# Gathers of tokens that fill all 128 partitions, in a transformer layer with a sorted mixture of experts

## The chip, the cores and the metric

The kernel runs on one core of one Trainium2 chip. The metric is device time in microseconds, from the start of the program to its end; the time before is the median of three runs. One further execution was taken by the hardware profiler, and all rows below come from it.

## The reference

Two transformer blocks follow each other on 512 tokens of 1024 features, all in float32. The first has an attention part (two kinds of heads) and a mixture of 32 experts; the second has another two kinds of attention. The part that matters here is the mixture:

```python
logits = (hf @ router_w + router_b)
top_val, top_idx = lax.top_k(logits, TOP_K)            # 4 of 32 experts for each token
gate = jax.nn.softmax(top_val, axis=-1)
...
u = hf[toks] @ w1[e] + b1[e]                           # 1024 -> 2048, for the tokens of expert e
g_, lin = u[:, :D_FF], u[:, D_FF:]
g_ = jnp.minimum(g_, SWIGLU_LIMIT)
lin = jnp.clip(lin, -SWIGLU_LIMIT, SWIGLU_LIMIT)
y = ((lin + 1.0) * g_ * jax.nn.sigmoid(SWIGLU_ALPHA * g_)) @ w2[e] + b2[e]   # 1024 -> 1024
return y * wts[:, None]
...
out = jax.ops.segment_sum(y.reshape(R, D), row_tok, num_segments=T)
```

For each expert its tokens are gathered, sent through two matrices, and added back into the rows that they came from.

## The kernel before

The first half of the program computes the attention of the first block, the router and, in `middle`, the lists of tokens of each expert. `h2d` is a table in DRAM with the normalised tokens (512 rows of 1024 numbers, 4 KB each), `accd` the one into which results are added.

**Experts.** Experts 0 and 1 come first; the other 30 are sorted by how many tokens they have, and the sorted order is dealt out so that small and large experts alternate (`KIND`, line 39): 15 small ones with up to 64 tokens ("S"), and 17 large ones ("L"). `SLOTS` (line 45) is the number of rows that an expert's tiles have: 64 for a small expert, 128 for the first two and the four largest of the others, 96 for the remaining 11 large ones. Tokens that do not fit go to `overflow`, a loop at the end that runs for no expert here.

**The stream of weights.** Every expert has 8 MB of first and 4 MB of second weights, loaded in pieces of 1024 KB by the SP queue (`Stream.pump`, line 135) into free blocks of SBUF. A load is issued as soon as a block is free, in the order in which the weights are used, so the queue runs ahead of the matmuls. Each piece for a large expert is split into two parts (a cast on ACT, line 167, and a subtraction on DVE, line 168) and used by three matmuls per tile (`mm3`, lines 257 to 259). A small expert's weights are used as they land, in full float32 matmuls that work on two halves of the output side by side (`pair`, line 1592).

**One expert.** The loop at line 1742 takes them in order. In the turn of expert e the kernel multiplies with the first weights of e (`up`), then with the second weights of e-1 (`down`). Between the pieces of `up` a hook runs: at the second piece the activations of e-1 are transposed (`turn_a`), at the fifth the gathered tokens of e+1 are transposed into the layout of the matmuls (`turn_x`), and right behind that the gather of expert e+2 is issued on GpSimd's queue (`gather`, line 1600) into the same tile `xg`. So a gather has about one expert's time until it is needed. At the end of `down` GpSimd issues a scatter that adds the result's rows to `accd` (line 1734 for large experts, whole rows; line 1705 for small ones, two halves of a row on 128 partitions).

**The gather before.** It reads whole rows of 4 KB, as many as the expert has slots, into as many partitions:

```python
ix = self.ig[0:n, c:c + 1] if large(e) else self.igs[0:n, c - NL:c - NL + 1]
nc.gpsimd.indirect_dma_start(out=xg[0:n, :], out_offset=None, in_=self.h2d[0:T, :], ...)
```

For a small expert `turn_x` then transposes eight pieces of 64 rows (line 1625) into one bank, which ACT copies to `small_x` with the eight pieces in order; `up` reads piece k at column 64 k. `igs`, the list of rows for small experts, is made once in `sorted_tables` (line 1495).

Of the kernel before, what the change touches and what calls it, by code (L numbers as in the profile page):

```python
# [14 lines left out]
OP = mybir.AluOpType  # L15
# [4 lines left out]
P = 128  # L20
T = 512
NT = 4
D = 1024
KD = 8
# [13 lines left out]
NL = E - 2 - NSMALL  # L38
# [6 lines left out]
SLOTS = [64 if KIND[_p] == "S" else P if _p < 2 or COL[_p] < NWIDE else 96 for _p in range(E)]  # L45
# [142 lines left out]
class Build:  # L188
# [1278 lines left out]
    def sorted_tables(self, pp):  # L1467

        nc = self.nc
        mm = nc.tensor.matmul  # L1470
        ns = E - 2
        y = pp.tile([P, D], F32, name="y", bufs=1)
        tu = self.sb_.cols(T, 2 * P)
        ones = self.halves[0:32, 0:1]

        def turned():
            nc.tensor.transpose(y[0:96, 0:P], self.tt, self.ident)
            nc.vector.tensor_copy(tu[0:96, 0:P], y[0:96, 0:P])
            nc.vector.tensor_copy(tu[0:96, P:].rearrange("p (h s) -> p h s", h=2),
                                  y[0:96, None, 0:64].to_broadcast([96, 2, 64]))  # L1480

        def by_rank():
            mm(y[:, 512:608], lhsT=tu[0:96, 0:P], rhs=self.bd[0:96, :], start=True, stop=True)
            mm(y[:, 608:704], lhsT=tu[0:96, P:], rhs=self.bd[0:96, :], start=True, stop=True)
            mm(y[0:1, 704:736], lhsT=self.pidf[0:32, :], rhs=self.bd[0:32, 0:E], start=True, stop=True)
            mm(y[0:1, 736:768], lhsT=ones, rhs=self.g[0:32, :], start=True, stop=True)
            nc.vector.tensor_copy(self.ids, y[0:1, 704:736])

        def lists():
            t, t2 = [y[:, a:a + 96].rearrange("p (c e) -> p c e", c=3) for a in (512, 608)]  # L1490
            f = self.sb_.cols(6 * T // 4 + 2 * E, NSMALL)

            nc.vector.tensor_scalar(f, t2[:, 1, NL:ns], -1.0, 1.0, op0=OP.mult, op1=OP.add)
            nc.vector.tensor_scalar(f, f, self.far2, self.half, op0=OP.mult, op1=OP.add)
            nc.vector.tensor_copy(self.igs, t2[:, 0, NL:ns])
            nc.vector.scalar_tensor_tensor(self.iscs, t2[:, 0, NL:ns], 2.0, f, op0=OP.mult, op1=OP.add)
            nc.vector.tensor_copy(self.gates, t2[:, 2, NL:ns])
            self.slots(t[:, 0, :NL], t[:, 1, :NL], t[:, 2, :NL], self.sb_.cols(6 * T // 4 + 3 * E, NL), self.ig[:, :NL],
                       self.isc[:, :NL], self.gate[:, :NL])

        def slots():
            r, a, b = [self.sb_[0:1, 6 * T // 4 + o:6 * T // 4 + o + E] for o in (0, E, 2 * E)]
            nc.vector.tensor_copy(r, y[0:1, 736:768])
            nc.vector.tensor_scalar(a, r, float(NL), -32.0, op0=OP.is_ge, op1=OP.mult)
            nc.vector.tensor_scalar(b, r, float(NWIDE), -32.0, op0=OP.is_ge, op1=OP.mult)
            nc.vector.tensor_tensor(out=a, in0=a, in1=b, op=OP.add)
            nc.vector.tensor_scalar(r, r, float(ns), 64.0, op0=OP.is_ge, op1=OP.mult)
            nc.vector.tensor_tensor(out=a, in0=a, in1=r, op=OP.add)
            nc.vector.tensor_scalar(a, a, 128.0, None, op0=OP.add)
            nc.vector.tensor_copy(self.cap, a)  # L1510
            nc.vector.tensor_tensor(out=a, in0=self.cntf[0:1, :], in1=a, op=OP.subtract)
            nc.vector.tensor_scalar(a, a, 0.0, None, op0=OP.max)
            nc.vector.tensor_copy(self.over, a)
            nc.vector.tensor_reduce(out=self.top, in_=a, axis=AX.X, op=OP.max)
        return [turned, by_rank, lists, slots]
# [30 lines left out]
    def experts(self):  # L1546
        nc, I, st, ar = self.nc, self.I, self.st, self.ar
        mm = nc.tensor.matmul
        with ExitStack() as cx:
# [18 lines left out]
            g_, l_ = [w[1].cols(q * D, D) for q in range(2)]  # L1568
            bb = self.bb
            sels = [bb.cols(FF + D // 2 + q * P, P) for q in range(3)]  # L1570
            accs = self.accd[:, :].rearrange("t (h n) -> (t h) n", h=2)

            def large(e):
                return KIND[e] == "L"
# [13 lines left out]
            def pair(out, lhsT, rhs, last):  # L1588

                for h in range(2):  # L1590
                    o = slice(64 * h, 64 * h + 64)
                    mm(out[o, :], lhsT=lhsT, rhs=rhs[:, h * 512:(h + 1) * 512], start=False, stop=last,  # L1592
                       tile_position=(0, 64 * h), skip_group_check=True)
            u_ = {}

            def gather(e):
                c = COL[e]
                n = SLOTS[e]
                ix = self.ig[0:n, c:c + 1] if large(e) else self.igs[0:n, c - NL:c - NL + 1]
                nc.gpsimd.indirect_dma_start(out=xg[0:n, :], out_offset=None, in_=self.h2d[0:T, :],  # L1600
                                             in_offset=bass.IndirectOffsetOnAxis(ap=ix, axis=0))

            def halves(e, at, H, L):
# [9 lines left out]
            a8 = s_.rearrange("p (j m o) -> p j o m", j=4, o=2)  # L1613
            a4 = s_[:, 0:T].rearrange("p (j m o) -> p j o m", j=2, o=2)

            def turn_x(e):
                def at(j):
                    return xg[:, j * P:(j + 1) * P]

                if large(e):  # L1620
                    halves(e, at, xH[e], xL[e])
                else:
                    p = pp.tile([P, D], F32, name="tr", bufs=1)
                    for j in range(KD):
                        nc.tensor.transpose(p[:, j * 64:j * 64 + 64], at(j)[0:64, :], self.ident[0:64, 0:64])
                    nc.scalar.copy(small_x, p[:, 0:T])
                self.select(sels[e % 3], e)

# [10 lines left out]
            def up(e, hook):  # L1639
                u = u_[e] = pp.tile([P, 2 * FF], F32, name="u", bufs=1)  # L1640
                m = SLOTS[e]
                if not large(e):
                    for b in range(2):
                        bias2(u[:, b * 512:(b + 1) * 512], e, b * 512)
                    for k, n in enumerate(self.e_w1[e]):
                        st.at = n
                        v = st.view(n)
                        for b in range(2):
                            pair(u[:, b * 512:(b + 1) * 512], small_x[:, k * 64:k * 64 + 64],
                                 v[:, 0, b * D:(b + 1) * D], k == KD - 1)  # L1650
                        st.free(n)
                        st.ahead(st.split_to)
                        hook(k)
                    return
                for c in range(4):
                    bias(u[0:m, c * 512:(c + 1) * 512], e, c % 2, (c // 2) * 512)
                for k in range(KD):
                    for h, p in enumerate(self.e_w1[e][k]):
                        st.at = st.pieces[p][0]
                        st.ahead(p)  # L1660
                        H, L = st.take(p)
                        for q in range(2):
                            c = 2 * h + q
                            s = slice(q * 512, (q + 1) * 512)
                            self.mm3(u[0:m, c * 512:(c + 1) * 512], xH[e][:, k, 0:m], xL[e][:, k, 0:m], H[:, 0, s],
                                     L[:, 0, s], False, k == KD - 1)
                        st.done(p)
                    hook(k)
# [14 lines left out]
            def down(e):  # L1683
# [4 lines left out]
                if not large(e):  # L1688
                    y = y[:, 0:T]
                    bias2(y, e, FF)  # L1690
                    for k in range(KD):
                        n = self.e_w2[e][k // 2]
                        st.at = n
                        o = (k % 4) * P + (k // 4) * 64
                        pair(y, small_a[:, o:o + 64], st.view(n)[:, k % 2, :], k == KD - 1)
                        if k % 2:
                            st.free(n)
                            st.ahead(st.split_to)
                        self.step()
                        if e == E - 2 and k == KD // 2:  # L1700
                            turn_a(E - 1)
                    ys = l_[:, 0:T]
                    c -= NL
                    nc.vector.scalar_tensor_tensor(ys, y, self.gates[:, c:c + 1], g2s, op0=OP.mult, op1=OP.mult)
                    nc.gpsimd.indirect_dma_start(
                        out=accs, out_offset=bass.IndirectOffsetOnAxis(ap=self.iscs[:, c:c + 1], axis=0), in_=ys,
                        in_offset=None, compute_op=OP.add)
                    return
# [720 lines left out]
```

## Time and profile before

| | us |
|---|---|
| median of three runs | 1778.27 |
| lowest and highest run | 1773.07, 1780.42 |
| the profiled execution | 1769.57 |
| its span in the trace | 1767.8 |
| TensorE (PE) busy in it | 1655.4 (94%) |
| DVE busy | 1101.6 (62%) |
| ACT busy | 847.1 (48%) |
| GpSimd (POOL) busy | 382.8 (22%) |

A busy TensorE is not one at its peak, since its matmuls are pipelined and overlap in the records. The profile's slices show in which part of the program each engine and the transfers are busy, its windows the same for any stretch, with the rate at which all transfers together moved bytes (GB/s) and the mean share in which the 16 DMA engines were busy; that share counts each packet's time and can read a little above 1 where packets overlap. The experts take the stretch from about 410 to 1475 us of the span.

### The profile page before, as it was taken

How to read it: one execution, taken by the hardware profiler on the slowest of the kernel's cores; microseconds unless marked ns; L12 is line 12 of the kernel's file. 1: busy time of each engine (PE TensorE's matmuls, PEld its weight loads, DVE VectorE, ACT ScalarE, POOL GpSimd, SP SyncE). 2: the span in 40 equal slices, each digit the busy share in tenths (PEclk: the TensorE clock that was granted, in tenths of full speed). 3: DMA queues.
4: the chain of work that ended last, by engine and by line, in shares of the span. 5: the costliest groups of instructions: out<-in, count | busy, mean ns of one | idle time of the engine just before them, and what ended most of it. 6: DMA issues, size and time to landing. Idle time of an engine off the chain costs nothing. (4 is left out here: it accounts for less than half of the span.)

```text
span 1767.8 us, 22276 instructions
## 1 busy us (share of the span) xinstructions
PE 1655.4 (94%) x8017; PEld 1066.5 (60%) x8018; DVE 1101.6 (62%) x1741; ACT 847.1 (48%) x1321; POOL 382.8 (22%) x259
## 2 busy tenths in 40 slices
PE   6999998897999999999999999999999989999998
PEld 4677755576775565464455464455455456778887
DVE  2567668669776475475485475476476486476653
ACT  4356568425554254254254255245245253477571
POOL 3013234222011121330321231231231130210120
PEclk9999999999999999999999999999999999999999
DMA  9802045457799999999999999999999996100301
GB/s 363 310 35 72 1 151 187 167 220 276 282 392 410 398 413 412 391 405 412 394 411 411 394 409 411 391 410 413 390 410 412 394 369 245 44 28 24 119 1 48
DMA packets 99656, 505.11 MB, mean 286 GB/s; under 512 B 10962, under 2 KB 20258, under 8 KB 48338
## 3 DMA queue, kind: packets, MB, share of 16 engines
q1 hardware_dynamic: 89972, 477.94, 67.3%
q0 software_dynamic: 8944, 24.63, 5.5%
q8 instruction: 65, 1.06, 0.2%
q10 hardware_dynamic: 624, 1.06, 0.2%
q14 instruction: 51, 0.42, 0.1%
HBM read 485.75 MB, written 17.84 MB: 285 GB/s over the span
## 5 line engine op out<-in xcount | busy, mean ns | idle before, releaser
L168 DVE TENSOR_TENSOR b<-b,b 128x1024 fp32r<-128x1024 f32 (+1 forms) x474 | 557.3, 1221 | 281.1 <-ACT b L167 280.4
L167 ACT CAST b<-b 128x1024 fp32r<-128x1024 f32 (+1 forms) x476 | 472.2, 1044 | 219.4 <-DMA b<-in_exp_w 175.9
L1734 POOL DMA_INDIRECT accd<-b,isc x16 | 162.1, 10130 | 440.7 <-DVE b L1729 440.7
L257 PE MATMUL z<-b,b 128*128 128x512 f32 (+1 forms) x544 | 224.9, 413 | 2.9 <-ACT b L167 2.1
L257 PE MATMUL u<-b,b 128*96 128x512 f32 (+1 forms) x560 | 224.5, 401 | 0.0
L259 PE MATMUL u<-b,b 128*96 128x512 f32 (+1 forms) x560 | 220.0, 393 | 0.0
L258 PE MATMUL u<-b,b 128*96 128x512 f32 (+1 forms) x560 | 219.8, 392 | 0.0
L1592 PE MATMUL u<-b,b 128*64 128x512 f32 x960 | 216.5, 597 | 0.8 <-DMA b<-in_exp_w 0.8
L258 PE MATMUL z<-b,b 128*128 128x512 f32 (+1 forms) x544 | 210.7, 387 | 1.5 <-DVE b L168 1.5
L259 PE MATMUL z<-b,b 128*128 128x512 f32 (+1 forms) x544 | 210.4, 387 | 0.0
L1592 PEld LDWEIGHTS u<-b,b 128*64 128x64 f32 x960 | 64.5, 136 | 122.1 <-issue 112.3
L257 PE MATMUL y<-b,b 128*96 128x512 f32 (+1 forms) x256 | 109.7, 428 | 23.6 <-ACT b L167 23.4
L258 PE MATMUL y<-b,b 128*96 128x512 f32 (+1 forms) x256 | 110.8, 433 | 20.2 <-DVE b L168 19.1
L257 PEld LDWEIGHTS z<-b,b 128*128 128x128 f32 x544 | 103.0, 189 | 33.5 <-issue 13.4
L257 PEld LDWEIGHTS u<-b,b 128*96 128x96 f32 (+1 forms) x560 | 96.0, 172 | 38.4 <-ACT b L167 5.7
L259 PEld LDWEIGHTS z<-b,b 128*128 128x128 f32 x544 | 102.7, 189 | 21.8 <-DVE b L1926 0.4
L259 PEld LDWEIGHTS u<-b,b 128*96 128x96 f32 (+1 forms) x560 | 95.8, 171 | 33.0
L258 PEld LDWEIGHTS u<-b,b 128*96 128x96 f32 (+1 forms) x560 | 96.0, 171 | 30.6
L258 PEld LDWEIGHTS z<-b,b 128*128 128x128 f32 x544 | 103.3, 190 | 16.2 <-DVE b L168 2.5
L1592 PE MATMUL y<-b,b 128*64 128x512 f32 x480 | 108.4, 604 | 0.0
L1609 ACT CAST b<-tr 128x768 fp32r<-128x768 f32 (+1 forms) x33 | 28.6, 867 | 164.0 <-PE tr L1607 164.0
L259 PE MATMUL y<-b,b 128*96 128x512 f32 (+1 forms) x256 | 106.6, 416 | 0.0
(516 smaller groups left out, 2109.1 us busy)
## 6 DMA issues: line engine op xcount, KB each, us to landing
b<-in_exp_w SPq DMA_DIRECT2D x384, 1024.0 KB, 20.2
b<-in_ada_w SPq DMA_DIRECT2D x24, 1024.0 KB, 6.8
b<-in_w_in SPq DMA_DIRECT2D x24, 1024.0 KB, 10.4
b<-in_w_out SPq DMA_DIRECT2D x8, 1024.0 KB, 5.0
b<-in_x SPq DMA_DIRECT2D x8, 512.0 KB, 6.7
b<-in_nsa_cmp_w POOLq DMA_DIRECT2D x2, 1024.0 KB, 9.1
b<-modd SPq DMA_DIRECT2D x4, 512.0 KB, 6.1
accd<-b SPq DMA_DIRECT2D x4, 512.0 KB, 3.4
```

The costliest lines, as they stand in the source:

```text
L167: nc.scalar.copy(hv, s)
L168: (other or nc.vector).tensor_tensor(out=lv, in0=s, in1=hv, op=OP.subtract)
L257: mm(out, lhsT=ah, rhs=bh, start=first, stop=False)
L258: mm(out, lhsT=ah, rhs=bl, start=False, stop=False)
L259: mm(out, lhsT=al, rhs=bh, start=False, stop=last)
L1592: mm(out[o, :], lhsT=lhsT, rhs=rhs[:, h * 512:(h + 1) * 512], start=False, stop=last, tile_position=(0, 64 * h), skip_group_check=True)
L1609: nc.scalar.copy(H[:, :, 0:n], pv)
L1734: nc.gpsimd.indirect_dma_start(out=self.accd, out_offset=bass.IndirectOffsetOnAxis(ap=self.isc[0:m, c:c + 1], axis=0), in_=ys[0:m, :], in_ ...
```

## The change

All gathers now write 128 partitions. A large expert always gathers 128 whole rows (of which the transposes go on using its 96 or 128 slots). A small expert gathers 128 half rows of 2 KB: partition p below 64 takes the first half of token p's row, partition 64 + p the second half, from `h2d` seen as 1024 half rows, with indices 2 x token + half. The gathered tile is then turned by four transposes of 128 rows, where eight of 64 rows were; the pieces lie in another order, which `up` reads through `small_at`, as `down` already did.

```diff
-            nc.vector.tensor_copy(self.igs, t2[:, 0, NL:ns])
+            nc.vector.tensor_scalar(self.igs, t2[:, 0, NL:ns], 2.0, self.half, op0=OP.mult, op1=OP.add)
...
-            accs = self.accd[:, :].rearrange("t (h n) -> (t h) n", h=2)
+            h2s, accs = [t[:, :].rearrange("t (h n) -> (t h) n", h=2) for t in (self.h2d, self.accd)]
...
             def gather(e):
                 c = COL[e]
-                n = SLOTS[e]
-                ix = self.ig[0:n, c:c + 1] if large(e) else self.igs[0:n, c - NL:c - NL + 1]
-                nc.gpsimd.indirect_dma_start(out=xg[0:n, :], out_offset=None, in_=self.h2d[0:T, :],
+                if large(e):
+                    out, src, ix = xg, self.h2d[0:T, :], self.ig[:, c:c + 1]
+                else:
+                    out, src, ix = xg[:, 0:T], h2s, self.igs[:, c - NL:c - NL + 1]
+                nc.gpsimd.indirect_dma_start(out=out, out_offset=None, in_=src,
                                              in_offset=bass.IndirectOffsetOnAxis(ap=ix, axis=0))
...
+            def small_at(t, k):
+                o = (k % 4) * P + (k // 4) * 64
+                return t[:, o:o + 64]
...
                     p = pp.tile([P, D], F32, name="tr", bufs=1)
-                    for j in range(KD):
-                        nc.tensor.transpose(p[:, j * 64:j * 64 + 64], at(j)[0:64, :], self.ident[0:64, 0:64])
+                    for j in range(4):
+                        nc.tensor.transpose(p[:, j * P:(j + 1) * P], at(j), self.ident)
                     nc.scalar.copy(small_x, p[:, 0:T])
...
-                            pair(u[:, b * 512:(b + 1) * 512], small_x[:, k * 64:k * 64 + 64],
+                            pair(u[:, b * 512:(b + 1) * 512], small_at(small_x, k),
                                  v[:, 0, b * D:(b + 1) * D], k == KD - 1)
...
-                        o = (k % 4) * P + (k // 4) * 64
-                        pair(y, small_a[:, o:o + 64], st.view(n)[:, k % 2, :], k == KD - 1)
+                        pair(y, small_at(small_a, k), st.view(n)[:, k % 2, :], k == KD - 1)
```

No instruction changes its place on any engine: the gathers, the transposes and the copy of the list stand where they stood, in other shapes and, for the transposes, half as many.

## Rows read from the trace of the kernel before

**Rows 1.** The page: the span, and DMA share and rate in 40 equal slices.
```profile
span 1767.8 us, 22276 instructions
...
PE   6999998897999999999999999999999989999998
...
DMA  9802045457799999999999999999999996100301
GB/s 363 310 35 72 1 151 187 167 220 276 282 392 410 398 413 412 391 405 412 394 411 411 394 409 411 391 410 413 390 410 412 394 369 245 44 28 24 119 1 48
```
**Rows 2.** Windows of 64 us: stretch, length, busy (instructions), clock, DMA share, GB/s.
```profile
526.00:590.00 64.00, 64.00 (x297) 40.67 (x296) 40.93 (x41) 28.51 (x30) 8.05 (x4) 1.00 1.02 406
590.00:654.00 64.00, 60.92 (x274) 36.10 (x274) 39.58 (x39) 28.08 (x30) 15.69 (x4) 1.00 1.02 416
846.00:910.00 64.00, 60.12 (x274) 32.20 (x274) 37.80 (x39) 27.62 (x30) 14.37 (x5) 1.00 1.02 404
```
**Rows 3.** Waits of TensorE's matmuls, 470 to 1440 us: total us, times, longest.
```profile
PE y L257 <- ACT b L167: 23.4, 17, 3.0
PE y L258 <- DVE b L168: 19.1, 30, 0.8
```
**Rows 4.** DMA issues, whole span: KB each, median us from issue to landing.
```profile
b<-in_exp_w SPq DMA_DIRECT2D x384, 1024.0 KB, 20.2
...
b<-h2d,ig POOLq DMA_INDIRECT x16, 11.0
```
**Rows 5.** Windows without an indirect transfer (columns as in rows 2).
```profile
834.00:848.00 14.00, 14.00 (x69) 9.89 (x68) 14.00 (x15) 8.95 (x11) 10.08 (x1) 1.00 1.01 428
898.00:916.00 18.00, 18.00 (x86) 12.74 (x85) 17.74 (x18) 11.39 (x13) 12.45 (x2) 1.00 1.01 426
```
**Rows 6.** DMA queues of the page: packets, MB, share of 16 engines.
```profile
q1 hardware_dynamic: 89972, 477.94, 67.3%
q0 software_dynamic: 8944, 24.63, 5.5%
```
**Rows 7.** Windows around gathers of 64 rows, the first and last of 14.
```profile
493.00:503.00 10.00, 10.00 (x47) 6.39 (x44) 6.91 (x10) 5.24 (x6) 0.00 (x0) 1.00 1.01 387
1336.00:1346.00 10.00, 7.68 (x30) 3.61 (x27) 4.04 (x4) 4.75 (x6) 0.00 (x0) 0.89 1.01 394
```
**Rows 8.** Windows around gathers of 128 whole rows that stand alone.
```profile
526.00:536.00 10.00, 10.00 (x47) 6.07 (x47) 5.36 (x6) 1.06 (x1) 0.00 (x0) 1.00 1.02 425
586.00:596.00 10.00, 10.00 (x46) 5.98 (x46) 5.36 (x5) 1.06 (x1) 0.00 (x0) 1.00 1.02 428
```
**Rows 9.** Windows around a scatter of 128 whole rows, and one of 128 half rows.
```profile
517.00:527.00 10.00, 10.00 (x49) 8.01 (x49) 8.27 (x9) 6.36 (x7) 0.99 (x1) 1.00 1.03 369
543.00:553.00 10.00, 10.00 (x54) 4.44 (x54) 4.35 (x4) 4.82 (x5) 0.92 (x1) 1.00 1.03 397
```
**Rows 10.** Windows around a scatter and gather together: 128+128, 128+96 twice, 96+96 twice.
```profile
652.00:666.00 14.00, 14.00 (x64) 6.77 (x64) 5.76 (x6) 1.06 (x1) 2.09 (x2) 1.00 1.02 386
718.00:732.00 14.00, 14.00 (x63) 6.45 (x63) 5.65 (x5) 1.06 (x1) 1.92 (x2) 1.00 1.02 358
784.00:798.00 14.00, 14.00 (x63) 6.25 (x63) 5.97 (x6) 1.06 (x1) 1.18 (x2) 1.00 1.03 359
851.00:865.00 14.00, 14.00 (x63) 6.04 (x63) 5.64 (x5) 1.06 (x1) 1.99 (x2) 1.00 1.02 373
1376.00:1390.00 14.00, 14.00 (x64) 6.28 (x64) 5.92 (x6) 1.06 (x1) 1.99 (x2) 1.00 1.03 360
```
**Rows 11.** TensorE's timeline, 700 to 740 us: start, us, line, shape.
```profile
704.10 0.63 PE L1636 MATMUL tr<-ident,b 128*128 128x128 f32 x4
...
712.86 0.71 PE L1625 MATMUL tr<-ident,b 64*128 64x64 f32 x8
...
739.87 0.88 PE L1607 MATMUL tr<-ident,b 96*128 96x96 f32 x8
```
**Rows 12.** GpSimd's timeline, 700 to 745 us.
```profile
716.81 1.54 POOL L1600 DMA_INDIRECT b<-h2d,ig  x1 [0.30 <-issue]
...
741.02 0.92 POOL L1600 DMA_INDIRECT b<-h2d,igs  x1 [9.14 <-PE tr L1607]
```

## The prediction

> **What bounds the kernel now.** I read the slices of the page first. From the twelfth slice to the thirty-third TensorE reads 9, but so does the DMA, at about 400 GB/s [rows 1]. The gathers are issued there, while 384 loads of expert weights stream in, so the question is which of the two sets the pace. The windows of 64 us (one large and one small expert together) tell: the DMA share is 1.02 in each, while TensorE has no idle time in the first, 3 us in the next and 4 us by 846 us [rows 2]. What TensorE waits for there is an ACT cast or a DVE subtraction, the first steps behind a landed weight, 42.5 us together [rows 3]. A weight load of 1024 KB takes 20.2 us from issue to landing [rows 4], while at the streaming rate it is only 2.5 us of work, so some eight loads stand in the queue and a buffer that comes free late starves nothing. The transfers set the pace.
>
> Next is the rate itself. In stretches without an indirect transfer it is 428 and 426 GB/s [rows 5]; I take 427. The indirect ones are costlier than their bytes: the software queue moved 24.63 MB in 5.5% of the span, 253 GB/s, the weights' queue 477.94 MB in 67.3%, 402 GB/s [rows 6]. So I price each indirect transfer by its **loss**: the length of a stretch around it, less the time that the weight bytes moved in it need at 427.
> - Gather of 64 rows: 14 stretches of 10 us, 387 GB/s in the first, 394 in the last [rows 7], mean 392.1. 3921 KB less the gather's 262 is 8.57 us of weights: loss **1.43 us**.
> - Gather of 128 rows: 425 and 428 [rows 8]; 4265 less 524 KB is 8.76 us: loss **1.24 us**. Twice the bytes cost less than the 64 rows.
> - Scatter of 128 whole rows: 369, loss 2.59 us. Scatter of 128 half rows: 397 in the first of 14, mean 393.9, loss 1.39 us [rows 9].
> - From the fourth pair on a scatter and a gather fall together, in 14 us. 128 rows and 128: 386, loss 3.80, the sum of 2.59 and 1.24. 128 rows scattered and 96 gathered: 358 and 359, loss 4.39. 96 and 96: nine stretches, 373 in the first and 360 in the last, mean 368.7, loss 3.75 [rows 10]. Taking off 2.59, or three quarters of it for 96 rows (1.94), leaves **1.80 us** for a gather of 96 rows, both ways.
>
> The prices can be tried on a whole pair: 25.17 MB of weights are 58.9 us, the losses 3.75, 1.43 and 1.39 make it 65.5 us, and with the indirect bytes that is 404 GB/s, which is what the window at 846 us reads [rows 2].
>
> **The change part by part.** *Large experts' gathers.* Five have 128 rows already. Eleven go from 96 to 128, all behind a scatter in the saturated stretch: from 1.80 to 1.24 us, 0.56 each, 6.2 us. The nearest rows are these same stretches, with 128 rows (3.80) beside 96 (4.39), which give 0.59. The other end is bytes alone: 32 rows more are 131 KB, 0.31 us each, 3.4 us lost.
>
> *Small experts' gathers.* Fifteen, of which the first runs while the stream is still filling; I count 14. No row shows 128 half rows gathered. Below stands half of the 128 whole rows, 0.62 us; above stands the scatter of the same shape, 1.39 us, which also reads and adds. I take 0.67: the scatters of half and whole rows stand as 1.39 to 2.59, and that ratio on 1.24 gives 0.67; it is a gather into all partitions, so that row is the nearer. The gain is 0.76 each, 10.6 us; at the ends 0.6 and 11.3.
>
> *TensorE.* Eight transposes of 64 rows, 0.71 us, become four of 128, 0.63 as in the other turn [rows 11]: 1.2 us over 15 experts, counted at nothing, since TensorE waits for the next weights in the same pair anyway.
>
> *GpSimd.* The small gather holds it 0.92 us, one of 128 rows about 1 to 1.6; in either place GpSimd stood idle or only behind its scatter. A gather issued at 716.81 lands 11.0 us later by the median, near 728, and is transposed at 739.87 [rows 4, 11, 12]: 12 us cover it. If that cover were gone, the turn and the matmuls behind it would wait. The one DVE copy of the index table becomes a multiply-add of the same shape, once: nothing.
>
> Sum: 6.2 + 10.6 = **16.8 us**. The profiled execution took 1769.57 us (span 1767.8), so it would take 1752.8. It lies 8.7 us below the median of the runs, 1778.27; against that median the forecast is **1761 us**, 0.9% faster. What is late next is still the weights: a pair falls to 64.2 us, while the TensorE idle time of 4 us in such a window [rows 2] covers the 1.3 us it loses. Behind the last expert nothing waits for a gather, so the rest moves forward whole.
>
> **The rivals.**
> 1. *Price by the fullest group of partitions.* 64, 96 and 128 rows all put whole rows into the first partitions, and if that group alone set the price, each would cost 1.24 us and only the half rows would gain: 14 x 0.62 = 8.7 us, 1769.6. For it: the 64 rows cost no less than 128. Against it: 1.43 and 1.80 are above 1.24 on average [rows 7, 10]. [...] Chance 0.12.
> 2. *Price by packets.* If two short packets keep the weights waiting as long as one of 4 KB does, the small gather costs what the half-row scatter does, 1.39, and gains 0.6 us in all; with the 6.2 of the large ones it is 1771.5. For it: 64 rows and 128 half rows, gathered and scattered, now cost nearly the same. Against it: the scatter's price halves with its row, 2.59 to 1.39 [rows 9], at the same number of packets. Chance 0.10.
> 3. *TensorE takes over.* Early there is no idle TensorE time [rows 2], and if buffers then held the loads back, half of the gain would be lost: 1770. Against it: loads stand eight deep, and only two of the small gathers lie before 590 us. Chance 0.05.
> 4. *Price by bytes: slower.* If a gather costs its bytes and what I read as imbalance belongs to the scatter beside it, small gathers stay as they are and eleven large ones cost 0.31 us more each: +3.4 us, 1781.7. It decides if the stretch with 96 and 128 rows reads no better than 373 GB/s. Against it: the 64 rows, alone in their stretch, lose more than 128. [...] Chance 0.05. That the change doesn't do what it says can be left out: every gather's shape is in its line.
>
> **How the numbers follow.** The forecast's own case has 0.68. The largest gain of its terms is 11.3 + 6.5 us; runs of the kernel before spread from 1773.07 to 1780.42, and I let the range reach from 1752 (the largest gain, and a low draw of the runs) to 1774, which takes in rivals 1 to 3 and leaves out the fourth. A measurement of this kernel can tell about 0.5%, 8.9 us, from no change, so faster means below 1769.4: the forecast's case and a part of rivals 1 and 3, together 0.75. Same: 0.21, the rest of these with rival 2 and the slower one at its price. Slower by over 0.5% needs more than any price here gives: 0.04.
>
> **What would show it.** The stretches of the small gathers should read about 425 GB/s where they read 392; those with 96 scattered and 128 gathered 395 where they read 369, in spite of more bytes. The distance between the same scatter of two neighbouring pairs should fall by the 1.3 us that the sum gives a pair. TensorE's idle time in the stage should shrink and its work stay; ahead of 420 us and behind the last expert nothing should move but the start. The prediction is wrong if the small gathers still read under 405, if the gather's loss moves into the scatter beside it, or if TensorE is found waiting for a gathered tile, at the eight or four transposes.

## The result and the profile after

| us | before | after |
|---|---|---|
| median of the runs | 1778.66 (4 runs, 1773.07 to 1780.42) | 1750.94 (4 runs, 1749.09 to 1753.14) |
| ratio, with its 95% interval | | 0.9856, 0.9835 to 0.9876 |
| the profiled execution | 1769.57 | 1751.53 |
| its span | 1767.8 | 1749.8 |

The change made the kernel 1.4% faster. Two differences stand in the table, and they are not the same: the traced executions are 18.0 us apart, the medians 27.7. The forecast was 16.8 us, taken off both: 1752.8 us for the profiled execution, which took 1751.53, and 1761 us for the median, which is 1750.94. Why the one came out and the other did not is what the experiments below are about.

The page of the changed kernel: the software queue moved more bytes than before (26.07 MB to 24.63) in a smaller share of a shorter span [rows 6].

```profile
span 1749.8 us, 22154 instructions
...
DMA  9712035456899999999999999999999986100301
GB/s 363 300 52 73 1 135 182 153 224 262 317 365 419 406 416 416 406 415 418 410 415 420 409 418 418 409 417 419 410 417 419 409 353 247 49 25 25 121 1 48
...
q0 software_dynamic: 9296, 26.07, 5.4%
```

Its windows, columns as in rows 2: the first and the last of the 14 small gathers, the first and last of nine stretches with 96 rows scattered and 128 gathered, and one pair of experts.

```profile
494.00:504.00 10.00, 10.00 (x46) 6.38 (x43) 6.91 (x10) 5.25 (x6) 0.00 (x0) 1.00 1.01 424
1322.00:1332.00 10.00, 8.45 (x31) 4.15 (x28) 5.53 (x6) 6.25 (x7) 0.00 (x0) 0.83 1.01 427
846.00:860.00 14.00, 14.00 (x64) 5.93 (x64) 5.63 (x5) 1.06 (x1) 2.04 (x2) 1.00 1.02 396
1361.00:1375.00 14.00, 14.00 (x65) 5.93 (x65) 5.63 (x5) 1.06 (x1) 2.05 (x2) 1.00 1.02 396
846.00:910.00 64.00, 60.73 (x274) 32.78 (x273) 39.08 (x39) 27.62 (x30) 15.56 (x5) 1.00 1.02 415
```

Against [rows 7, 10, 2]: the small gathers' stretches read 426.8 GB/s in the mean of 14, where they read 392.1; the nine others 395.2, where they read 368.7; the pair 415, where it read 404. By the reckoning of the prediction (427 GB/s, the gather's bytes taken off) a small gather now loses 10 - (4268 - 262) / 427 = **0.62 us**, and a scatter of 96 with a gather of 128 rows 14 - (5533 - 917) / 427 = 3.19, where it was 3.75. 0.62 us is no more than the time that the gather's own 262 KB need at 427 GB/s.

The packets of the two traces show one more thing. A gather of 128 half rows is recorded as 64 packets of 4 KB, as the gather of 64 whole rows was: the software queue has 352 packets more than before, and these are the 32 rows more of each of eleven large gathers. But a packet of a small gather now takes 159 ns (median, in each of the 14), where it took 177 to 226.

GpSimd's timeline shows the distance of eight pairs, from one scatter of half rows to the same one eight pairs on, first in the kernel before:

```profile
863.43 1.57 POOL L1705 DMA_INDIRECT accd<-b,iscs  x1 [12.01 <-DVE b L1704]
1389.11 1.57 POOL L1705 DMA_INDIRECT accd<-b,iscs  x1 [12.01 <-DVE b L1704]
```

and in the changed one:

```profile
858.24 1.58 POOL L1710 DMA_INDIRECT accd<-b,iscs  x1 [11.78 <-DVE b L1709]
...
1373.34 1.59 POOL L1710 DMA_INDIRECT accd<-b,iscs  x1 [11.88 <-DVE b L1709]
```

525.7 us became 515.1: 65.7 a pair before, 64.4 after, 1.3 us less.

TensorE's waits in the stage (470 to 1440 us), to be held against [rows 3], fell from 42.5 to 37.0 us in all:

```profile
PE y L258 <- DVE b L168: 19.5, 31, 0.8
PE y L257 <- ACT b L167: 17.5, 20, 1.9
```

### The profile page after: what moved, and what is told of

Its sections match the earlier page's. It is cut to its first block, busy times and chain, and to the rows that moved or that the text cites. A ratio compares the mean times of both kernels' runs of the same rounds, so it can differ in the third digit from the quotient of the medians.

```text
span 1749.8 us, 22154 instructions
## 1 busy us (share of the span) xinstructions
PE 1641.9 (94%) x7957; PEld 1059.2 (61%) x7958; DVE 1100.6 (63%) x1741; ACT 847.0 (48%) x1321; POOL 383.4 (22%) x259
## 3 DMA queue, kind: packets, MB, share of 16 engines
q0 software_dynamic: 9296, 26.07, 5.4%
## 5 line engine op out<-in xcount | busy, mean ns | idle before, releaser
L258 PE MATMUL y<-b,b 128*96 128x512 f32 (+1 forms) x256 | 107.6, 420 | 21.0 <-DVE b L168 19.5
L257 PE MATMUL y<-b,b 128*96 128x512 f32 (+1 forms) x256 | 105.3, 411 | 17.5 <-ACT b L167 17.5
L259 PEld LDWEIGHTS z<-b,b 128*128 128x128 f32 x544 | 102.7, 189 | 21.8 <-DVE b L1931 0.4
L259 PE MATMUL y<-b,b 128*96 128x512 f32 (+1 forms) x256 | 103.5, 404 | 0.0
```

The lines of the kernel that those rows point to most:

```text
L257: mm(out, lhsT=ah, rhs=bh, start=first, stop=False)
L258: mm(out, lhsT=ah, rhs=bl, start=False, stop=False)
L259: mm(out, lhsT=al, rhs=bh, start=False, stop=last)
```

## The experiments

All ratios are to the kernel before, run beside it on the same chip: 23 runs for runs 1 to 4 (median 1776.82 us, from 1765.03 to 1785.03), 13 for runs 5 to 8 (1774.94, from 1770.89 to 1780.72). Gains in us are worked out from the ratio; the difference of the two medians is up to 3 us larger.

**1. The large experts' part alone.**

```diff
-                n = SLOTS[e]
+                n = P if large(e) else SLOTS[e]
```

> Only the large experts' part of the change: they gather 128 whole rows, small ones still 64. My prices (a gather is costly when its rows fill the partitions unevenly) expect 11 x 0.56 = 6.2 us off, so a ratio near 0.9965, and the stretches with a scatter of 96 rows and a gather at 395 GB/s. Price by the fullest group of partitions: nothing, 369 to 371 GB/s less the added bytes' place. Price by bytes: 3.4 us slower, ratio 1.002.

Measured: 0.9968 (0.9938 to 0.9998), 1768.41 us, ten runs from 1763.16 to 1777.18. The nine stretches read 394.8 GB/s in the mean; the first and the last of them, and a stretch behind a small gather:

```profile
848.00:862.00 14.00, 14.00 (x63) 6.21 (x63) 5.66 (x6) 1.06 (x1) 2.04 (x2) 1.00 1.02 393
1374.00:1388.00 14.00, 14.00 (x64) 6.29 (x64) 5.91 (x6) 1.06 (x1) 2.04 (x2) 1.00 1.02 397
...
1338.00:1361.00 23.00, 20.18 (x79) 12.87 (x80) 19.45 (x21) 16.58 (x18) 0.00 (x0) 0.93 1.01 372
```

More bytes in less time: the price of 96 rows was real, and the gain is 5.7 us where 6.2 were reckoned. The interval of the ratio is wide (0.4 to 11 us), so it is the stretches that decide: 394.8 GB/s where they read 368.7. The price by bytes falls, as does the price by the fullest group, which gave this part nothing. The last line is a new thing: 23 us behind a gather of 64 rows, with no indirect transfer in them, and yet the stream runs at 372 GB/s.

**2. The small experts' part alone.**

```diff
-                    out, src, ix = xg, self.h2d[0:T, :], self.ig[:, c:c + 1]
+                    n = SLOTS[e]
+                    out, src, ix = xg[0:n, :], self.h2d[0:T, :], self.ig[0:n, c:c + 1]
```

(The diff is to the changed kernel.)

> Only the small experts' part: 128 half rows, large ones still gather 96 whole rows. My prices: 14 x 0.8 = 11 us off by the profile, ratio near 0.994. If the whole change is worth 27.7 us because something else than the lost transfer time goes away with the eight transposes or the 64 rows, most of those 27.7 should appear here, ratio 0.988 or below; if the two parts only add up beyond their prices together, neither run shows it.

Measured: 0.9911 (0.9879 to 0.9943), 1758.26 us, six runs from 1754.21 to 1759.08. That is 15.8 us, 4 to 5 more than the gathers' own prices, and lies between the two ratios of the expectation. The runs lie close together, which those of run 1 and of the kernel before do not. The two parts add up to 21.5 us by their ratios (27.0 by medians), about as much as the whole change gives (25.6 by the ratio of the result, 21.8 by that of run 8), so no gain beyond the two parts is seen. The same pair of experts as above:

```profile
846.00:910.00 64.00, 60.27 (x272) 32.54 (x271) 38.59 (x39) 27.12 (x30) 15.05 (x5) 1.00 1.02 410
```

**3. The kernel before, traced again.**

> The kernel before, unchanged. The change took 18.0 us off the span of the profiled execution but 27.7 us off the median of the runs. If the profiled execution of before was only a fast draw, this one's profile should lie at 1773 to 1780 us and show where the extra 5 to 10 us of a usual run are: in the stage of the experts (more loss per gather, then they belong to the change) or elsewhere (then they are chance). If profiling itself makes it faster, it lies at 1770 again.

Measured: 0.9992 (0.9967 to 1.0017); its profiled execution is slower than the first, the span is 1776.1 us. Up to 480 us its windows read the same rates as those of the first trace. In the stage the difference shows, below as a window of 20 us behind one of the gathers of 64 rows:

```profile
885.00:905.00 20.00, 17.46 (x65) 10.89 (x66) 16.65 (x18) 15.08 (x17) 0.00 (x0) 0.91 1.01 373
```

The first trace reads 426 a little later in the same pair [rows 5]. In this stretch a weight packet of 8 KB takes 352 ns in the median, where 309 is usual, though the gather's last packets go out at its very start and the next scatter is issued only at 908 us; after 27 us the pace comes back. I counted such **slow stretches** in each trace (microseconds between 460 and 1450 us in which the median packet of 8 KB takes 330 to 420 ns, four or more in a row): 14 us in the first trace of before, 75 in this one. (The count moves by some us, up to 8 in a trace, with where the microseconds begin.) At 374 instead of 427 GB/s a slow microsecond loses 0.12 us, so the 61 more cost 7.6 us of the 8.3 that the spans differ.

**4. The same 64 whole rows, in partitions 32 to 95.**

```diff
+                s = slice(0, SLOTS[e]) if large(e) else slice(32, 96)
-                nc.gpsimd.indirect_dma_start(out=xg[0:n, :], ...
+                nc.gpsimd.indirect_dma_start(out=xg[s, :], ...
...
-                        nc.tensor.transpose(p[:, j * 64:j * 64 + 64], at(j)[0:64, :], self.ident[0:64, 0:64])
-                    nc.scalar.copy(small_x, p[:, 0:T])
+                        nc.tensor.transpose(p[:, j * P:(j + 1) * P], at(j), self.ident)
+                    nc.scalar.copy(small_x.rearrange("p (j m) -> p j m", m=64),
+                                   p.rearrange("p (j m) -> p j m", m=P)[:, :, 32:96])
```

> Small experts gather the same 64 whole rows of 4 KB, but into partitions 32 to 95 instead of 0 to 63 (turned by eight transposes of 128 rows, of which the copy takes the 64 columns that hold tokens). Theory 1, the price is uneven partitions: these 64 lie half on either side of partition 64, so each loses about 0.65 us where 1.43 were lost, and 10 to 11 us go without any row having become shorter. Theory 2, the price is the length or the number of rows: no gain, loss 1.43 each, 392 GB/s in the stretches of 10 us.

Measured: 0.9905 (0.9876 to 0.9935), 1758.31 us, as much as the small experts' part of the change, with whole rows, as many rows and as many bytes as before. Its stretches read 426.0 GB/s in the mean of 14, a loss of 0.64 us, with a median of 159 ns for its packets as in the changed kernel; the first and one from the middle:

```profile
495.00:505.00 10.00, 10.00 (x46) 6.32 (x43) 6.91 (x10) 5.24 (x6) 0.00 (x0) 1.00 1.01 421
1003.00:1013.00 10.00, 6.99 (x27) 3.07 (x24) 4.51 (x4) 5.34 (x6) 0.00 (x0) 0.89 1.01 427
```

What a small gather loses beyond the time of its bytes hangs on where the rows land: neither the length nor the number of the rows has changed here.

**5. Small experts gather 128 whole rows**, each token twice.

```diff
-                n = SLOTS[e]
+                n = SLOTS[e] if large(e) else P
```

> Small experts gather 128 whole rows (each token twice, the second copy unused), twice the bytes of before; large ones as before. Theory 1 (even partitions): 1.24 us each where 1.43 were lost, 2.7 us less in the gathers, and no stretch of the stream at the slow pace of about 376 GB/s that the traces of before show behind some gathers of 64 rows, so the runs should lie close together and below those of before. Price by bytes: 0.61 us more for each of 14, 8.6 us slower.

Measured: 0.9948 (0.9929 to 0.9967), four runs from 1763.46 to 1766.33. With twice the bytes the gather is cheaper: 425.9 GB/s in the mean of 14 stretches with 524 KB in each, 1.25 us.

```profile
493.00:503.00 10.00, 10.00 (x46) 6.53 (x43) 6.92 (x8) 5.24 (x6) 0.00 (x0) 1.00 1.02 425
1005.00:1015.00 10.00, 7.10 (x26) 2.98 (x23) 3.39 (x3) 4.11 (x5) 0.00 (x0) 0.88 1.02 428
```

Each gather costs the time of its bytes at 427 GB/s (1.23 us) and hardly more. The prices give 2.5 us of the 9.2 measured. The rest would be the slow stretches that a usual run of before has, of which this trace has some 10 us.

**6. Half rows, but in partitions 0 to 63**, two gathers side by side.

```diff
+                if not large(e):
+                    src = self.h2d[:, :].rearrange("t (h n) -> (t h) n", h=2)
+                    for q, t in enumerate((self.igs, self.igs2)):
+                        nc.gpsimd.indirect_dma_start(
+                            out=xg[0:n, q * T:(q + 1) * T], out_offset=None, in_=src, ...
```

(`igs` holds 2 x token, `igs2` 2 x token + 1.)

> Small experts gather half rows of 2 KB, as in the change, but both halves into partitions 0 to 63, side by side, by two gathers; eight transposes as before. Theory 1: uneven as before, loss 1.4 to 1.6 us for the two together and slow stretches, no faster than before. Theory 2 (short rows help): loss 0.65 us and the gain of the small experts' part, ratio 0.991.

Measured: 1.0056 (1.0039 to 1.0074), slower than before. 376.1 GB/s in the mean of 14, 1.81 us for the two:

```profile
494.00:504.00 10.00, 10.00 (x47) 6.39 (x44) 6.91 (x10) 5.24 (x6) 0.34 (x1) 1.00 1.01 369
1014.00:1024.00 10.00, 5.68 (x24) 1.94 (x23) 2.03 (x2) 2.62 (x3) 0.64 (x1) 1.00 1.02 380
...
905.00:920.00 15.00, 15.00 (x73) 10.63 (x72) 15.00 (x16) 9.96 (x12) 10.00 (x1) 1.00 1.01 421
```

Half rows in one half of the partitions help nothing, and the two gathers lose more than the 1.4 to 1.6 us expected. Here too the trace records 64 packets of 4 KB for them (median 206 ns over the 14); whether the rest of the loss comes of issuing two gathers was not tried. That there were no stretches at 374 I had not expected. But from the first of the 14 small gathers on, the stream keeps to a slightly lower pace through almost the whole stage: 421 GB/s in the last line, with a median of 312 ns for its 8 KB packets where 309 is usual, and no faster behind the large gathers (422 and 424 in 9 us from 535 and 594 us on; the first trace of before reads 428 and 431 there). The first loads of that trace, ahead of any gather, show 312 ns as well, so it is open whether the small gathers cause this pace.

**7. The 64 whole rows in partitions 64 to 127.** Run 4 with one number changed.

```diff
-                s = slice(0, SLOTS[e]) if large(e) else slice(32, 96)
+                s = slice(0, SLOTS[e]) if large(e) else slice(64, 128)
...
-                                   p.rearrange("p (j m) -> p j m", m=P)[:, :, 32:96])
+                                   p.rearrange("p (j m) -> p j m", m=P)[:, :, 64:128])
```

> The kernel with 64 whole rows in partitions 32 to 95, with one number changed: they go to partitions 64 to 127. Theory 1: one half of the partitions again, loss 1.4 us and more, slow stretches, ratio to before 1.00. If instead partitions 0 to 31 were the costly ones, or the eight transposes of 128 rows made the gain, it stays at 0.9905.

Measured: 1.0007 (0.9981 to 1.0034), ten runs from 1767.69 to 1789.51. The price is back, 392.3 GB/s in the mean of 14 and 1.43 us, and so are the slow stretches (40 us):

```profile
491.00:501.00 10.00, 10.00 (x46) 6.36 (x43) 6.91 (x10) 5.24 (x6) 0.00 (x0) 1.00 1.01 385
1008.00:1018.00 10.00, 7.79 (x29) 3.49 (x26) 3.98 (x4) 4.69 (x6) 0.00 (x0) 0.83 1.01 396
```

So neither half is at fault, and the larger transposes of run 4 gave nothing. Run 2, with four transposes, and run 4, with eight, gain the same (0.9911 and 0.9905): TensorE's part of the change is worth nothing that can be measured, as the prediction had it.

**8. The changed kernel again.**

> The changed kernel again, for a second trace. If slow stretches of the stream come from gathers that fill one half of the partitions, this trace has none, the weights' 8 KB packets keep to one pace between the indirect transfers, and the runs lie within 0.3% of each other; ratio 0.985. If the first trace was a lucky draw, some stretch here reads 376 GB/s.

Measured: 0.9877 (0.9856 to 0.9899), four runs from 1747.31 to 1753.69, a span of 1745.6 us, and no slow stretch, as in the first trace after. The runs spread by 0.36%, a little more than the 0.3% expected. The pair of experts in this trace, and, from the first trace after, a stretch behind a small gather like that of run 3:

```profile
846.00:910.00 64.00, 60.73 (x275) 32.84 (x273) 39.02 (x40) 27.62 (x30) 15.61 (x4) 1.00 1.02 415
```

```profile
885.00:902.00 17.00, 15.55 (x68) 10.17 (x68) 16.26 (x17) 14.46 (x16) 4.83 (x1) 1.00 1.01 423
```

**9 and 10. Two more traces of the kernel before.**

> The kernel before, one more trace, to test whether the slow stretches of the weight stream (about 375 GB/s where 427 is usual, behind gathers of 64 rows) make its runs differ. Theory: the span is that of the first trace, 1767.8 us, plus 0.12 us for each us of slow stretch that this trace has more. Rival: the spans differ for other reasons, and a slow span comes with few slow stretches or the reverse.

> As the run before it, a fourth trace of the kernel before: span 1767.8 us plus 0.12 us for each us of slow stretch beyond those of the first trace, to within 2 us.

These two ran on another chip than runs 1 to 8. The slow stretches of each trace, and the span that the theory gives for them:

| trace of before | slow stretches, us | span, us | span by the theory |
|---|---|---|---|
| first | 14 | 1767.8 | |
| run 3 | 75 | 1776.1 | 1775.1 |
| run 10 | 99 | 1776.5 | 1778.0 |
| run 9 | 105 | 1780.1 | 1778.7 |

All within 2 us. One slow stretch of run 9 and one of run 10:

```profile
1353.00:1374.00 21.00, 19.99 (x81) 13.00 (x82) 18.56 (x21) 15.13 (x17) 0.00 (x0) 0.93 1.01 376
```

```profile
1016.00:1040.00 24.00, 21.29 (x82) 13.80 (x83) 20.07 (x22) 17.23 (x19) 0.04 (x1) 0.86 1.01 373
```

## Why the prediction was right, and where it fell short

*What bounds the kernel.* Right. The DMA share stays at 1.02, and what each gather loses less is gained whole: 1.3 us a pair was forecast, 1.3 is what the scatters' distances show. (One of the slices was misread: TensorE's thirty-third is an 8 and not a 9, on which nothing rests.)

*The small gathers.* 0.67 us was taken, between 0.62 and 1.39; measured 0.62, the lower end. Half the bytes cost half of what 128 whole rows cost. The term is 14 x (1.43 - 0.62) = 11.3 us, where 10.6 were summed.

*The large gathers.* 0.56 us was taken; 3.75 less 3.19 is 0.56. To share the loss of 3.75 between scatter and gather, three quarters of 2.59, 1.94, had been assumed for the scatter of 96 rows; now that the gather beside it has 128 rows and costs 1.24, 3.19 leaves 1.95 for it. Run 1 measures 5.7 us for this part as a whole, the sum had 6.2.

Together 17.5 us, and the traced executions differ by 18.0. The mechanism and its two terms held.

*What failed is the step from the trace to the median*: "It lies 8.7 us below the median of the runs", after which I took the 16.8 us off that median as if the distance would stay. It was no fixed distance. The first trace was a lucky draw with few of the slow stretches, and so neither the trace nor the sum could hold them. In the four traces of before they are 14 to 105 us, 73 in the mean, at 0.12 us some 9 us; in the two after there are none. 17.5 and 9 make 26.5, and the medians differ by 27.7. The size of this second part is known less well than the first: run 8, the same comparison again, has 23.6 us between the medians, which leaves it 6. The median lies 1 us below the range of 1752 to 1774 (the ratio, taken on the 1778.27 us of the prediction, gives 1752.7), whose lower end was the largest gain of the terms off the one fast trace; that the forecast of the traced execution came so near, 1752.8 for 1751.53, owes something to that trace being nearly free of slow stretches. The hint stood in the table of times: the trace was faster than each run shown, by 3.5 to 10.9 us, in a kernel that the change then steadied to 1747 to 1754 (eight runs).

*The rivals.* The fullest group (8.7 us): fallen as the whole price, since 96 rows lose more than 128 and run 1's stretches gain. Run 4 does not speak against it: if the groups are the two halves of the partitions, 32 of its rows lie in each, and this rival too would give half of 1.24 us, 0.62, where 0.64 was measured. That it matters how the rows lie on the halves is what runs 4 and 7 show, with 0.64 us against 1.43 for the same rows; why it matters, no run shows. By the fuller half alone 96 rows would cost no more than the 1.24 us of 128, as both fill the first half, and the trace has 1.80; why is open, since no run laid 96 rows elsewhere. The price by packets: its number fell, the half rows cost their bytes; but they were recorded as 64 packets of 4 KB, so what shorter packets would cost was not tried. The price by bytes: fallen, run 5 moved twice the bytes in less time; bytes alone are the price of a gather that fills both halves evenly (0.62 us for 262 KB, 1.25 for 524). TensorE taking over: fallen, it still waits 37.0 us and the pairs became shorter by the whole 1.3 us.

*What was to be seen.* The rates forecast for the two kinds of stretches were 425 and 395 GB/s; they are 426.8 and 395.2. One expectation was wrong: TensorE's waits were to shrink and its work to stay, but its busy time fell too, from 1655.4 to 1641.9 us. Busy time is no measure of work here: the window at 1322 us above, with 1.55 us of idle time in it, has a granted clock of 0.83 (0.50 in the 3.3 us from 1328.4 us on, 1.00 in the 6.3 us before), while those without idle time have 1.00. A matmul of line 257 takes 628 ns in those 3.3 us, in the median, and some 392 ns at 1.00. The mean over the span is 0.980 in the first trace before and 0.987 in the first one after; 0.7% of 1655 us is 11.6 us, an estimate from these two means, and the 60 transposes fewer, counted at 1.2 us, make up most of the rest. That the shorter waits raised the clock fits, but no run shows it, and the window from 871 to 881 us of the same trace, with as much idle time, has 1.00.

No run beat the changed kernel. Runs 4 and 5 suggest no better one: the even gather of 64 whole rows costs as much as that of half rows.

## What to carry to other kernels

Where a stream of large loads sets the pace, price every other transfer by the bytes of the stream that it displaces, not by its own duration or size: 64 rows of 4 KB cost more here than 128 as long as they landed in one half of the partitions (1.43 us against 1.24), and 0.64 us across both. Spread a small transfer over both halves (more partitions with shorter rows, or merely rows that lie across partition 64). And when one trace lies outside the spread of the runs, take a second trace before trusting either: what differs between the two may be a good part of the effect, here about a third.

## What the runs showed of the hardware that was not expected

An uneven gather can leave the stream of loads at a lower steady pace after it is over: 373 to 376 GB/s where 427 is usual, for up to some 30 us and with nothing else in flight, behind some gathers of 64 rows in one half of the partitions and not behind others. Five of the six traces with such a gather of whole rows show it, 40 to 105 us in all, a few of these behind gathers of 96 rows; the sixth, the first of before, has 14 us, all behind gathers of 96 rows. Where the small gathers lie evenly and the large ones still have 96 rows it is some 4 to 14 us (runs 2, 4 and 5), where all gathers fill 128 partitions none (two traces). With two gathers of half rows in one half there were none either, but a milder slowing, to 421 GB/s, through almost the whole stage (run 6). Why the stream stays in that state, and what ends it, was not tried.

Of the 14 small gathers of a trace, the median packet of 4 KB took 159 ns in every one that was spread evenly over both halves (the changed kernel, runs 2, 4 and 5), and 170 ns and more in every one that was not, with medians of 206 to 214 over a trace (the kernel before, runs 3, 6 and 7).
